# A gMLP and SwiGLU layer on one core: tiles moved to multiples of 512 bytes in SBUF, with the split weights' slots 64 bytes apart in the line

## The chip, the cores and the metric

The kernel runs on one core of one Trainium2 chip. What counts is the device time of one execution in microseconds (us). Kernels are compared by the median of several executions.

## The reference

One layer with batch 1, sequence 2048 and model width 1024, in float32. A conditioning vector c gives shifts, scales and gates.

```
mod = silu(c) @ mod_w + mod_b
sh1, sc1, g1, sh2, sc2, g2 = split(mod, 6)
h = x * (1 + sc1) + sh1
z = gelu(h @ w_in + b_in); u, v = split(z, 2); v = layer_norm(v)
sv = einsum('gts,bnsgc->bntgc', tril(w_s), chunks of 128 of v) + b_s
y = (u * sv) @ w_out
x = layer_norm(2 ** 0.25 * x + (1 + g1) * y)
h = x * (1 + sc2) + sh2
g, u = split(h @ ffn_w_in, 2); y = (silu(g) * u) @ ffn_w_out        (hidden width 2816)
x = layer_norm(2 ** 0.25 * x + (1 + g2) * y)
```

## The kernel before

Every large product is carried in float32 by three passes. An operand is split into two float32r parts, hi and lo, and hi*hi + hi*lo + lo*hi is added up in PSUM. The split is `parts` (lines 85 to 90): ScalarE (ACT) casts the float32 source into the first half of a tile (line 88), VectorE (DVE) writes source minus first half into the second half (line 89). Such a tile has the shape `UNIT`, 4096 bytes a partition; `ROW` is 4096 bytes too, `HALF` 2048. Each matmul reads two such tiles from SBUF: the stationary operand, 128 columns by 128 rows, which a weight load brings in ahead, and the moving operand, 512 columns.

The mixer goes over four blocks of 512 tokens (`b` = 0 to 3) in three stages:

- `v_part` (`token_major`, line 192): the stationary operand is `hT`, on the right side of SBUF, the moving one the split weight `wv`, in the pool `w` on the left.
- `us_part` (`feature_major`, line 209): the stationary operand is `wu` (pool `w`, left), the moving one `hT` (right). Between them stand the short spatial products (line 310) and the transposes (line 382).
- `y_part` (`token_major`, line 192): the stationary operand is `yT`, the moving one `wo` (pool `w`). Both are on the left.

The feed-forward part takes Winograd's form, seven products for a 2x2 one. In `ffn_in` (line 428) the split weights of the pool `w` (left) are stationary and the activations move: A11 and A12 lie on the right, the five others (A22, S1 to S4) on the left. `ffn_in` goes twice over 11 pairs (`f_0` to `f_10`, each with a `g` and a `u` half); a pair has 14 products of 12 matmuls. In `ffn_out` (`mm`, line 577) the moving operand is the split `wd` (pool `w`, or `fin` for the last product, where it lies left), the stationary one the split `al`: for the first half of the tokens in the pool `w` on the right, for the second half in `w2` on the left.

A pool stands for one tag of `phase` (lines 61 to 68). It is a stack with a left side, which grows from the low addresses, and a right side, which grows down from the top:

```
            p = st.enter_context(tc.tile_pool(name=f"{tag}{n[0]}", bufs=bufs, side=side, reuse_waits="tile"))
```

```
    late = phase("left", late=(12, ROW))
    mix = phase("left", w=(7, UNIT), cact=(1, ROW))
    early = phase("right", hT=(8, UNIT), u=(5, HALF), xh=(2, HALF), sv=(2, HALF))
    rest = phase(
        "left", s=(4, HALF), opsS4=(2, UNIT), opsS2=(4, UNIT), h3=(4, ROW), c=(8, HALF), w=(6, UNIT), opsS1=(4, UNIT),
    )
    most = phase("right", ld=(9, HALF), w=(10, UNIT))
```

All slots are multiples of 512 bytes, so all of these tiles on one side have the same place in a line of 512 bytes. That place is 64 on the left and 480 on the right; it follows from the small tiles that are allocated first, and the pads of the change show it (64 + 448 and 480 - 480 are multiples of 512). When a phase ends, its bytes are used again, and `reuse_waits="tile"` makes a new tile wait for the old tiles whose bytes it covers. A scheduler that simulates the program then sets the order of the instructions on each engine; each engine works through its own in order. All loads and stores are issued from SyncE's queue (SP).

Of the kernel before, what the change touches and what calls it, by code (L numbers as in the profile page):

```python
# [8 lines left out]
F32 = mybir.dt.float32  # L9
# [4 lines left out]
P = 128  # L14
# [4 lines left out]
NT = TB // P  # L19
ND = D // P  # L20
NK = ND // 2
NP = 11
ALPHA = 2.0 ** 0.25
EPS = 1e-5

# Winograd's form of the 2x2 product C = A B in seven products:
#   P1 = A11 B11   P2 = A12 B21   P5 = S1 T1   P6 = S2 T2   P3 = S4 B22   P7 = S3 T3   P4 = A22 T4
#   S1 = A21 + A22   S2 = S1 - A11   S3 = A11 - A21   S4 = A12 - S2
#   T1 = B12 - B11   T2 = B22 - T1   T3 = B22 - B12   T4 = B21 - T2
#   C11 = P1 + P2         C12 = P1 + P6 + P5 + P3  # L30
#   C21 = P1 + P6 + P7 + P4   C22 = P1 + P6 + P7 + P5
A_OF = {1: "A11", 2: "A12", 3: "S4", 4: "A22", 5: "S1", 6: "S2", 7: "S3"}
# [4 lines left out]
def gmlp_swiglu_layer(  # L37
# [6 lines left out]
):  # L44
    """One gMLP + SwiGLU layer.

    Every large product is float32 carried as three one-pass products: an operand is the exact
    sum of two float32r parts (12 significant bits each), hi and lo, and hi*hi + hi*lo + lo*hi
    is accumulated in float32. The products of the feed-forward part take Winograd's form.
    """  # L50
    nc = tc.nc
# [4 lines left out]
    dram = ctx.enter_context(tc.tile_pool(name="dram", bufs=1, space=bass.MemoryType.DRAM))  # L56

    ROW, HALF, UNIT = ([P, D], F32), ([P, 512], F32), ([P, 2, 512], F32R)
    cur, n = {}, [0]

    def phase(side, **tags):
        """Open one pool for each tag: tag=(number of slots, shape and type). Close what is returned."""
        st = ExitStack()
        for tag, (bufs, kind) in tags.items():
            n[0] += 1
            p = st.enter_context(tc.tile_pool(name=f"{tag}{n[0]}", bufs=bufs, side=side, reuse_waits="tile"))
            cur[tag] = (p, kind)
        return st

    def new(tag, name, kind=None):  # L70
        p, (shape, dt) = cur[tag][0], kind or cur[tag][1]
        return p.tile(shape, dt, tag=tag, name=name)

    lo, hi = slice(0, 512), slice(512, 1024)
# [10 lines left out]
    def parts(src, name, tag):  # L85
        """[P, 512] float32 as its hi and lo parts."""
        o = new(tag, name, UNIT)
        nc.scalar.copy(out=o[:, 0, :], in_=src)  # L88
        nc.vector.tensor_tensor(out=o[:, 1, :], in0=src, in1=o[:, 0, :].bitcast(F32), op=ALU.subtract)  # L89
        return o  # L90
# [7 lines left out]

    # constants
    ident = const.tile([P, P], F32, name="ident")  # L100
# [5 lines left out]

    # conditioning: mod = silu(c) @ mod_w + mod_b, one column per 128 outputs
    modc = const.tile([P, 48], F32, name="modc")
# [29 lines left out]
    def spread(k, name):  # L138
        """Columns [P, 1] * ND as one row on every partition, by way of DRAM."""
        line = dram.tile([ND, P], F32, name=f"{name}_line")  # L140
        nc.sync.dma_start(out=line.rearrange("d p -> p d"), in_=modc[:, k * ND : (k + 1) * ND])
        t = new("late", name)
        nc.sync.dma_start(out=t, in_=line.rearrange("d p -> (d p)").partition_broadcast(P))
        return t
# [4 lines left out]
    def norm_of(st, name):  # L149
        """Mean and 1 / sqrt(var + EPS)."""  # L150
        mv = small.tile([P, 2], F32, tag="mv", name=f"{name}_mv")
        nc.vector.bn_aggr(out=mv, in_=st)
        ve = small.tile([P, 1], F32, tag="ve", name=f"{name}_ve")
        nc.vector.tensor_scalar(ve, mv[:, 1:2], EPS, None, ALU.add)  # L154
        rs = small.tile([P, 1], F32, tag="rs", name=f"{name}_rs")
        nc.gpsimd.tensor_tensor(out=rs, in0=ve, in1=mhalf, op=ALU.pow)  # L156
        # one Newton step: rs * (1.5 - 0.5 * ve * rs^2)
        nw = small.tile([P, 1], F32, tag="nw", name=f"{name}_nw")
        nc.vector.scalar_tensor_tensor(out=nw, in0=rs, scalar=ve, in1=rs, op0=ALU.mult, op1=ALU.mult)
        nc.vector.tensor_scalar(nw, nw, -0.5, 1.5, ALU.mult, ALU.add)  # L160
        nc.vector.tensor_tensor(out=rs, in0=rs, in1=nw, op=ALU.mult)
        return mv[:, 0:1], rs
# [10 lines left out]
    def ahead(makers, depth=2):  # L173
        """The makers' results in order; each is made `depth` uses before its own."""
        made = [m() for m in makers[:depth]]

        def results():
            for i in range(len(makers)):
                if i + depth < len(makers):
                    made.append(makers[i + depth]())  # L180
                yield made[i]

        return results()

    def token_major(operands, nk, name, between=()):
        """out[t, :] over NT token tiles: sum over k of a_k[:, t].T @ w_k, in all 8 banks."""
        ps = [[bank(f"{name}_ps{t}{h}") for h in range(2)] for t in range(NT)]
        for k, (a, w) in enumerate(operands):
            for t in range(NT):
                for part, wpart in HL:  # L190
                    for h in range(2):
                        nc.tensor.matmul(  # L192
                            ps[t][h],
                            lhsT=a[:, part, t * P : (t + 1) * P],
                            rhs=w[h][:, wpart, :],
                            start=(k == 0 and part == 0 and wpart == 0),
                            stop=(k == nk - 1 and part == 1),
                        )
            for f in between[k :: nk]:
                f()  # L200
        return ps

    def feature_major(w, rhs, name):
        """out[j, tokens] of 128 features: w is [d, (d-tile, j)] in parts."""
        ps = bank(name)
# [13 lines left out]
    x1d = [dram.tile([TB, D], F32, name=f"x1d{b}") for b in range(NB)]  # L219
    # left operands of the feed-forward products, [k, tokens of one half] in float32  # L220
    hop = [[[dram.tile([P, TB], F32, name=f"hop{o}_{k}_{sb}") for sb in range(2)] for k in range(NK)] for o in range(7)]
# [8 lines left out]
    sh1, sc1, g1, sh2, sc2, g2 = ([None] * ND for _ in range(6))  # L230
    env = {}

    def setup_spatial():
        # masked w_s, transposed to [s, (g, t)]
        wm = new("bcv", "wm")
# [3 lines left out]
            out=wm3, in_=wm3,  # L239
            pattern=[[0, 8], [1, P]], compare_op=ALU.is_ge, fill=0.0, base=0, channel_multiplier=-1,  # L240
        )
        # tb[c, (g, t)] = ln_b[c] * sum_s w[t, s] + b_s[g, t]
        lb = new("raw", "lnb_bc")
# [122 lines left out]
    def h2_part(b, i, cols_of, tag):  # L366
        """Transposed, modulated feature tiles i and NK + i; with the second half of a super-block their left operands.

        cols_of(t, q) is token tile t's columns of feature tile i + q * NK.
        """  # L370
        sb = b // 2
# [28 lines left out]
    def a_operands(r0, r1, name):  # L400
        """Raw [k0, (t0, t1)] and [k1, (t0, t1)] -> S1..S4 and the seven left operands in float32."""
        a11, a21, a12, a22 = r0[0], r0[1], r1[0], r1[1]
# [7 lines left out]
    def load_ops(sb, names):  # L410
        def tag_of(n, k):
            """A22, S3 and most of S4 take rows that the mixer leaves."""
            return "late" if n in ("A22", "S3") or (n == "S4" and k > 1) else "ops" + n

        out = {}
# [8 lines left out]
    def ffn_in(sb, ops, between={}):  # L424
# [12 lines left out]
        def weight(fp, pr, gu):  # L437
# [6 lines left out]
            b11, b12, b21, b22 = B[gu]  # L444
            # T1, T2 take the place of B11, T3 of B12, T4 of B21
            if pr == 5:
# [13 lines left out]
        for fp in range(NP):  # L460
            X, Y, Z, c1, u1, u2 = {}, {}, {}, {}, {}, {}
            for pr in order:
# [30 lines left out]
                if (fp, pr) in between:  # L493
                    between[fp, pr]()
            # C11 in c1, C12 in u1, C22 in u2, C21 in X
            for cc in (c1, u2, u1):
# [8 lines left out]
    def residual(b, t, r, cs, st, scaled=False):  # L505
        """r * (1 + g2) + alpha * x1 on half a row, with its sums."""
        xt = new("xr", f"xr{b}_{t}_{cs.start}")[:, : cs.stop - cs.start]
# [10 lines left out]
    def finish(b, t, r, st, e):  # L518
        """Norm and store of one token tile; `e` adds, or none where the wait for it would be the longest."""
        row = b * TB + t * P  # L520
# [15 lines left out]

    # token tile pairs: (sb, p) joins tile p of the first and of the second half of sb
    prs = [(sb, p) for sb in range(2) for p in range(NT)]
# [44 lines left out]
    def ffn_out():  # L583
# [29 lines left out]

        # P3 adds to P5 and P6, P7, P4 to P1 where they accumulate; the last product of the second half
        # comes pair by pair, so that each pair's norm follows at once
        steps = [(pr, k) for pr in (2, 5, 3, 1, 6, 7, 4) for k in range(NP)]
# [153 lines left out]
```

## Time and profile before

| | |
|---|---|
| median of 3 executions | 1949.47 us |
| fastest, slowest | 1949.44 us, 1951.29 us |
| span of the profiled execution, first to last instruction | 1948.5 us |
| median less the span: what lies around it | 1.0 us |
| TensorE (PE) busy | 1875.5 us, 96% of the span |
| DVE, ACT, GpSimd (POOL) busy | 66%, 39%, 37% |
| DMA queue of SP | 47.2% of 16 engines |

The page of the profile takes one execution, and gives no time of its own but the span. A busy PE is not one at its peak: matmuls follow each other in a pipeline, so the distance from one start to the next is what a matmul costs, and the chain of work that ended last gives it, as a run's time by its number of matmuls.

### The profile page before, as it was taken

The page shows a single profiled execution, that of the slowest core. Times are in us where ns is not written, and L with a number is a line of the kernel's source. Part 1 is how long each engine was busy: PE and PEld are TensorE (multiplying, and loading weights), DVE is VectorE, ACT ScalarE, POOL GpSimd, SP SyncE. Part 2 cuts the span into 40 slices and gives each one's busy share as a digit, 9 for nine tenths or more (in the row PEclk, how much of TensorE's full clock was granted, in tenths as well). Part 3 has the DMA queues.
Part 4 walks back from the last instruction along what each step waited for, and adds up shares of the span by engine and source line. Part 5 has one row for each costly group of instructions (what it writes and reads, how often), then busy time and mean ns, then how long its engine had stood idle before and what let it go on. Part 6 is the DMA issues. An engine that isn't in the chain of part 4 may idle for free.

```text
span 1948.5 us, 23471 instructions
## 1 busy us (share of the span) xinstructions
PE 1875.5 (96%) x8297; PEld 1532.5 (79%) x8297; DVE 1284.1 (66%) x1855; ACT 760.2 (39%) x1251; POOL 716.6 (37%) x465
## 2 busy tenths in 40 slices
PE   7999999999999999999999999999999999999776
PEld 6787788778888788888887888888888888887655
DVE  8486866786758856555668566556554433476998
ACT  3432552543545434333345333333343443332321
POOL 0000500550402666645544554355431200244834
PEclk9999999999999999999999999999999999999978
DMA  9358546464455444542236323322347644555542
GB/s 355 121 184 304 170 153 229 156 226 155 141 184 184 140 157 152 173 142 97 103 117 195 121 102 106 108 91 103 113 145 246 215 130 140 168 172 172 191 151 108
DMA packets 135064, 312.77 MB, mean 161 GB/s; under 512 B 16641, under 2 KB 21025, under 8 KB 134946
## 3 DMA queue, kind: packets, MB, share of 16 engines
q1 hardware_dynamic: 134882, 311.24, 47.2%
q8 instruction: 65, 1.06, 0.2%
q14 instruction: 53, 0.43, 0.1%
q0 software_dynamic: 64, 0.03, 0.0%
HBM read 239.37 MB, written 71.84 MB: 160 GB/s over the span
## 4 chain that ended last, share of the span: by engine, by line
PE 80%; DVE 11%; DMA 4%; issue 2%; POOL 1%; ACT 1%; SPq 0%; DVEq 0%; POOLq 0%; ACTq 0%
PE o L577 18%; PE v_ps L192 8%; PE u_ps L209 7%; PE y_ps L192 6%; PE f_4u_X L428 1%; PE f_2u_X L428 1%; PE f_5u_X L428 1%; PE f_3u_X L428 1%; PE f_8u_X L428 1%; PE f_7u_X L428 1%; PE f_6u_X L428 1%; PE f_8g_X L428 1%; PE f_7g_X L428 1%; PE f_6g_X L428 1%; PE f_3g_X L428 1%
## 5 line engine op out<-in xcount | busy, mean ns | idle before, releaser
L577 PE MATMUL o<-wd_w,alw 128*128 128x512 f32 (+1 forms) x1881 | 434.4, 393 | 33.3 <-DVE o L77 28.2
L577 PEld LDWEIGHTS o<-wd_w,alw 128*128 128x128 f32 x1881 | 352.8, 191 | 114.8 <-ACT alw L88 23.5
L192 PE MATMUL v_ps<-wv,hT 128*128 128x512 f32 x768 | 184.8, 402 | 16.7 <-ACT wv L88 11.8
L89 DVE TENSOR_TENSOR alw<-al,alw 128x512 fp32r<-128x512 f32 x154 | 130.1, 877 | 98.0 <-ACT alw L88 97.8
L192 PEld LDWEIGHTS v_ps<-wv,hT 128*128 128x128 f32 x768 | 147.1, 192 | 53.5 <-ACT wv L88 12.1
L209 PE MATMUL u_ps<-hT,wu 128*128 128x512 f32 x768 | 186.5, 402 | 1.8 <-DVE v L281 1.3
L192 PE MATMUL y_ps<-wo,yT 128*128 128x512 f32 x768 | 175.7, 390 | 1.9 <-DVE sv L315 1.9
L209 PEld LDWEIGHTS u_ps<-hT,wu 128*128 128x128 f32 x768 | 144.9, 191 | 36.9 <-issue 1.9
L192 PEld LDWEIGHTS y_ps<-wo,yT 128*128 128x128 f32 x768 | 143.7, 188 | 32.3 <-issue 1.8
L156 POOL TENSOR_TENSOR ln_rs<-ln_ve,mhalf 128x1 f32<-128x1 f32 x32 | 27.8, 876 | 361.2 <-DVE ln_ve L154 349.9
L88 ACT CAST alw<-al 128x512 fp32r<-128x512 f32 x154 | 88.8, 618 | 149.2 <-PE o L577 121.6
L89 DVE TENSOR_TENSOR wu<-wu_raw,wu 128x512 fp32r<-128x512 f32 x64 | 65.8, 1042 | 53.6 <-ACT wu L88 53.5
L80 POOL TENSOR_TENSOR chain<-wd,chain 128x512 f32<-128x512 f32 x22 | 33.7, 1532 | 159.4 <-DVE wd_w L89 127.2
L88 ACT CAST wv<-wv_raw 128x512 fp32r<-128x512 f32 x64 | 37.5, 619 | 106.0 <-PE v_ps L192 43.2
L118 DVE SCALAR_TENSOR_TENSOR modw<-modw,cact 128x1024 f32<-128x1024 f32 x48 | 58.3, 1217 | 19.9 <-DMA modw<-in_modwT 19.9
L89 DVE TENSOR_TENSOR wv<-wv_raw,wv 128x512 fp32r<-128x512 f32 x64 | 47.4, 759 | 22.4 <-ACT wv L88 22.2
L89 DVE TENSOR_TENSOR wo<-wo_raw,wo 128x512 fp32r<-128x512 f32 x64 | 46.4, 732 | 20.4 <-ACT wo L88 20.2
L89 DVE TENSOR_TENSOR wd_w<-wd,wd_w 128x512 fp32r<-128x512 f32 x44 | 34.8, 791 | 37.0 <-ACT wd_w L88 37.0
L88 ACT CAST wo<-wo_raw 128x512 fp32r<-128x512 f32 x64 | 38.6, 616 | 43.5 <-PE y_ps L192 42.1
L88 ACT CAST wu<-wu_raw 128x512 fp32r<-128x512 f32 x64 | 38.2, 616 | 36.1 <-PE v_ps L192 20.8
L88 ACT CAST wd_w<-wd 128x512 fp32r<-128x512 f32 x44 | 27.2, 619 | 48.1 <-PE o L577 36.0
L359 POOL TENSOR_TENSOR r<-r,ln1g_bc 128x1024 f32<-128x1024 f32 x16 | 41.5, 2611 | 11.5 <-ACT r L168 11.5
(604 smaller groups left out, 3879.7 us busy)
## 6 DMA issues: line engine op xcount, KB each, us to landing
al<-aop SPq DMA_DIRECT2D x154, 256.0 KB, 3.2
wd<-in_wd SPq DMA_DIRECT2D x99, 256.0 KB, 3.2
modw<-in_modwT SPq DMA_DIRECT2D x48, 512.0 KB, 8.4
aop<-aop_s SPq DMA_DIRECT2D x88, 256.0 KB, 2.0
wv_raw<-in_wv SPq DMA_DIRECT2D x32, 512.0 KB, 4.6
wu_raw<-in_wu SPq DMA_DIRECT2D x32, 512.0 KB, 4.3
wo_raw<-in_wo SPq DMA_DIRECT2D x32, 512.0 KB, 3.5
hop<-h SPq DMA_DIRECT2D x40, 256.0 KB, 3.1
```

The source lines that it names most:

```text
L80: nc.gpsimd.tensor_tensor(out=o, in0=a, in1=b, op=ALU.subtract)
L88: nc.scalar.copy(out=o[:, 0, :], in_=src)
L89: nc.vector.tensor_tensor(out=o[:, 1, :], in0=src, in1=o[:, 0, :].bitcast(F32), op=ALU.subtract)
L118: nc.vector.scalar_tensor_tensor(out=w, in0=w, scalar=1.0, in1=env["cact"], op0=ALU.mult, op1=ALU.mult, accum_out=modc[:, j : j + 1],)
L156: nc.gpsimd.tensor_tensor(out=rs, in0=ve, in1=mhalf, op=ALU.pow)
L192: nc.tensor.matmul(ps[t][h], lhsT=a[:, part, t * P : (t + 1) * P], rhs=w[h][:, wpart, :], start=(k == 0 and part == 0 and wpart == 0), sto ...
L209: nc.tensor.matmul(ps, lhsT=w[d // 4][:, wpart, (d % 4) * P : (d % 4 + 1) * P], rhs=rhs[d][:, part, :], start=(n == 0), stop=(n == 3 * ND ...
L359: nc.gpsimd.tensor_tensor(out=r, in0=r, in1=env["ln1g"], op=ALU.mult)
L428: nc.tensor.matmul(ps, lhsT=w[:, wpart, k * P : (k + 1) * P], rhs=a[k][:, part, :], start=(first and k == 0 and wpart == 0 and part == 0), ...
L577: nc.tensor.matmul(ps[:, cs], lhsT=a[:, part, p * P : (p + 1) * P], rhs=w[:, wpart, cs], start=(first and part == 0 and wpart == 0), stop= ...
```

## The change

Two pads are allocated ahead of the phases' pools, 448 bytes on the left and 480 on the right, and filled once by DVE. With them the two sides begin at 0 modulo 512. A slot of a pool with the tag `w` grows from 4096 to 4160 bytes, of which the first 4096 are used; its seven (mixer), six (`ffn_in`) and ten (`ffn_out`) slots so lie 0, 64, 128, ... bytes into the line. The pools `w2` and `fin` keep their slots. Tiles behind the pool `w` on its side are moved by its number of slots times 64 bytes: 448 for the mixer's `yT`, `raw`, `bcv` and `vrow`, 384 for `opsS1`. The scratch of the software DMA queue goes from its default of 16384 bytes to 4096, a multiple of 512 less. Comments are taken out; lines from 58 on have other numbers (88 and 89 become 99 and 100, 428 becomes 439).

```diff
+    for side, pad in (("left", 448), ("right", 480)):
+        pads = ctx.enter_context(tc.tile_pool(name=f"pad_{side}", bufs=1, side=side))
+        nc.vector.memset(pads.tile([P, pad // 4], F32, name=f"pad_{side}"), 0.0)
...
     def new(tag, name, kind=None):
         p, (shape, dt) = cur[tag][0], kind or cur[tag][1]
+        if (shape, dt) == UNIT and tag in STEP:
+            t = p.tile([P, 2 * 512 + STEP[tag] // 4], dt, tag=tag, name=name)
+            return t[:, : 2 * 512].rearrange("p (h c) -> p h c", h=2)
         return p.tile(shape, dt, tag=tag, name=name)
+
+    STEP = {"w": 64}
...
-    nc = bacc.Bacc("TRN2", target_bir_lowering=False, num_devices=1)
+    nc = bacc.Bacc("TRN2", target_bir_lowering=False, num_devices=1, dynamic_dma_scratch_size=4096)
```

The matmuls, splits and transfers are the same in number and size. In the built programs' addresses, of 7,881 float32r matmuls those whose two operands differ in their place modulo 512 bytes are:

| | matmuls | before: differ | by | after: differ | by |
|---|---|---|---|---|---|
| v | 768 | 768 | 416 | 648 | 128 to 448 in steps of 64 |
| u | 768 | 768 | 96 | 648 | 64 to 384 |
| y | 768 | 0 | | 768 | 64 to 448 |
| ffn_in | 3696 | 1056 | 96 | 3168 | 64 to 448 |
| ffn_out | 1881 | 1014 | 96, 416 | 1566 | 64 to 448 |
| sum | 7881 | 3606 | | 6798 | |

("By" is the stationary operand's place less the moving one's, modulo 512.)

The order moves in one place only, from the mixer's last product to the first pairs of `ffn_in`, where slots of 4160 bytes lie over other old tiles than before. ACT there, before (`wo_7` is the last weight of the mixer; `h2S` are S1 to S4, whose raw tiles end in the product's name and the feature tile, as `h2S1r_0`; `f_0g_w` is a split weight of the first pair):

```order
393 L88 CAST h2S_0_0_5289<-h2S1r_0_5287 128x512
394 L88 CAST h2S_0_1_5294<-h2S1r_1_5292 128x512
395 L88 CAST wo_7_1_5133<-wo_7_raw 128x512
396 L88 CAST f_0g_w_5331<-f_0g_b_5327 128x512
397 L88 CAST h2S_0_2_5299<-h2S1r_2_5297 128x512
398 L88 CAST f_0u_w_5338<-f_0u_b_5334 128x512
399 L88 CAST f_0g_w_5341<-f_0g_b_5328 128x512
400 L88 CAST f_0u_w_5344<-f_0u_b_5335 128x512
401 L88 CAST h2S_0_3_5304<-h2S1r_3_5302 128x512
402 L88 CAST f_0g_w_5348<-f_0g_b_5327 128x512
403 L88 CAST f_0u_w_5367<-f_0u_b_5334 128x512
404 L88 CAST h2S_0_0_5309<-h2S2r_0_5307 128x512
```

ACT there, after:

```order
393 L99 CAST h2S_0_0_5299<-h2S1r_0_5297 128x512
394 L99 CAST h2S_0_1_5304<-h2S1r_1_5302 128x512
395 L99 CAST wo_7_1_5143<-wo_7_raw 128x512
396 L99 CAST h2S_0_2_5309<-h2S1r_2_5307 128x512
397 L99 CAST h2S_0_3_5314<-h2S1r_3_5312 128x512
398 L99 CAST h2S_0_0_5319<-h2S2r_0_5317 128x512
399 L99 CAST h2S_0_1_5324<-h2S2r_1_5322 128x512
400 L99 CAST f_0g_w_5341<-f_0g_b_5337 128x512
401 L99 CAST f_0u_w_5348<-f_0u_b_5344 128x512
402 L99 CAST f_0g_w_5351<-f_0g_b_5338 128x512
403 L99 CAST f_0u_w_5354<-f_0u_b_5345 128x512
```

The first pair's weights stood ahead of the casts from `h2S2r` (the raw tiles of S2) and now stand behind two of them. The tile that the second of these writes covers part of the slot of `wo_7_0`. PE there, before, with all twelve matmuls of a product together:

```order
1972 L192 MATMUL y_ps_4967<-wo_7_1_5133,yT_7_4925 128x512
1973 L428 MATMUL f_0g_X<-h2A_0_0_5210,f_0g_w_5331 128x512 x3
1974 L428 MATMUL f_0g_X<-h2A_0_1_5215,f_0g_w_5331 128x512 x3
1975 L428 MATMUL f_0g_X<-h2A_0_2_5220,f_0g_w_5331 128x512 x3
1976 L428 MATMUL f_0g_X<-h2A_0_3_5225,f_0g_w_5331 128x512 x3
1977 L428 MATMUL f_0u_X<-h2A_0_0_5210,f_0u_w_5338 128x512 x3
```

PE there, after:

```order
1972 L203 MATMUL y_ps_4977<-wo_7_1_5143,yT_7_4935 128x512
1973 L439 MATMUL f_0g_X<-h2A_0_0_5220,f_0g_w_5341 128x512 x2
1974 L439 MATMUL f_0u_X<-h2A_0_0_5220,f_0u_w_5348 128x512 x2
1975 L439 MATMUL f_0g_Y<-h2A_0_0_5240,f_0g_w_5351 128x512 x2
1976 L439 MATMUL f_0g_X<-h2A_0_0_5220,f_0g_w_5341 128x512
1977 L439 MATMUL f_0g_X<-h2A_0_1_5225,f_0g_w_5341 128x512 x3
1978 L439 MATMUL f_0g_X<-h2A_0_2_5230,f_0g_w_5341 128x512 x3
1979 L439 MATMUL f_0g_X<-h2A_0_3_5235,f_0g_w_5341 128x512 x3
1980 L439 MATMUL f_0u_Y<-h2A_0_0_5240,f_0u_w_5354 128x512 x2
```

The matmuls that need only the hi part of a weight are now taken out of three products and put ahead, since the lo parts come later: on DVE they stand behind the eight multiplications that empty the mixer's banks (line 343 before, 354 after), where the first six stood ahead of them.

## Rows read from the trace of the kernel before

**Rows 1.** The page: span, busy PE, the chain that ended last.

```profile
span 1948.5 us, 23471 instructions
PE 1875.5 (96%) x8297; PEld 1532.5 (79%) x8297; DVE 1284.1 (66%) x1855; ACT 760.2 (39%) x1251; POOL 716.6 (37%) x465
PE 80%; DVE 11%; DMA 4%; issue 2%; POOL 1%; ACT 1%; SPq 0%; DVEq 0%; POOLq 0%; ACTq 0%
```

**Rows 2.** Chain in order of time, mixer: start us, us, what, number.

```profile
274.29 43.55 PE y_ps L192 x192
...
465.86 44.80 PE v_ps L192 x192
510.65 22.50 PE u_ps L209 x96
...
566.29 43.32 PE y_ps L192 x191
```

**Rows 3.** Chain, `ffn_in`, second time, pair 6 and the start of pair 7.

```profile
1281.45 2.81 PE f_6u_X L428 x12
1284.26 2.81 PE f_6g_Y L428 x12
1287.08 2.80 PE f_6u_Y L428 x12
...
1292.62 2.72 PE f_6u_Z L428 x12
1295.35 2.72 PE f_6g_X L428 x12
...
1319.95 2.81 PE f_7u_X L428 x12
```

**Rows 4.** Stretches: us, busy by engine, PEclk (granted clock), DMA share, GB/s.

```profile
319.00:359.00 40.00, 40.00 (x174) 32.16 (x173) 36.65 (x76) 13.54 (x20) 14.26 (x8) 1.00 0.62 214
...
570.00:606.00 36.00, 36.00 (x160) 29.84 (x159) 21.35 (x28) 15.96 (x29) 7.33 (x5) 1.00 0.56 177
1283.00:1450.00 167.00, 167.00 (x730) 136.80 (x729) 98.22 (x105) 60.91 (x104) 80.61 (x52) 1.00 0.32 110
```

**Rows 5.** Groups on ACT: the casts of line 88, busy us, mean ns.

```profile
L88 ACT CAST alw<-al 128x512 fp32r<-128x512 f32 x154 | 88.8, 618 | 149.2 <-PE o L577 121.6 <-DMA al<-aop 18.0 <-issue 6.6
L88 ACT CAST wo<-wo_raw 128x512 fp32r<-128x512 f32 x64 | 38.6, 616 | 43.5 <-PE y_ps L192 42.1 <-PE u_ps L209 1.3
L88 ACT CAST yT<-sv 128x512 fp32r<-128x512 f32 x32 | 19.9, 621 | 48.0 <-DVE sv L322 48.0
```

**Rows 6.** Chain, `ffn_out`: its long stretches of PE, and one between them.

```profile
1477.81 293.32 PE o L577 x1270
...
1814.41 2.89 DVE alw L89
...
1866.42 41.51 PE o L577 x164
```

**Rows 7.** Timeline, end of the mixer: start us, us, engine, line, instruction.

```profile
596.04 0.68 DVE L89 TENSOR_TENSOR f_0g_w<-f_0g_b,f_0g_w 128x512 fp32r<-128x512 f32 x1
...
604.88 0.68 DVE L89 TENSOR_TENSOR f_0u_w<-f_0u_b,f_0u_w 128x512 fp32r<-128x512 f32 x1
605.56 5.37 DVE L343 TENSOR_TENSOR r<-y_ps,g_bc 128x512 f32<-128x512 f32 x8
605.96 0.62 ACT L88 CAST h2S<-h2S2r 128x512 fp32r<-128x512 f32 x1 [3.78 <-DMA h2S2r<-hop]
...
609.66 2.97 PE L428 MATMUL f_0g_X<-h2A,f_0g_w 128*128 128x512 f32 x12
```

**Rows 8.** Waits of PE from 600 to 720 us: us in total, times, longest.

```profile
PE f_1u_Y L428 <- DVE f_1u_w L89: 3.0, 1, 3.0
PE f_1g_Y L428 <- DVE f_1g_w L89: 0.9, 1, 0.9
PE f_1g_Y L428 <- ACT f_1g_w L88: 0.8, 1, 0.8
```

**Rows 9.** Chain, the first piece: what the start waits for.

```profile
2.20 7.67 DMA xT<-in_xT
```

## The prediction

> **What bounds the kernel now.** The page comes first: PE is busy 96% of the span, and 80% of the chain that ended last is PE's own work [rows 1]. So the next question is what one matmul costs inside a stretch where PE waits for nothing. The chain in order of time gives it, as a run's time by its number of matmuls. The reader should see two prices there, and no third. In `y`, where both operands lie on the left, 192 matmuls take 43.55 us, or 226.8 ns each, and 191 take 43.32, again 226.8 [rows 2]. In `v` it is 44.80 / 192 = 233.3 ns and in `u` 22.50 / 96 = 234.4 ns [rows 2]; there one operand is on the right. `ffn_in` has both prices side by side, in one loop: the products with A11 and A12, whose activations lie on the right, take 2.81 us for twelve (234.2 ns), those with S1 to S4 and A22 take 2.72 us (226.7 ns) [rows 3]. [...]
>
> What goes with the price? In the dear matmuls the stationary and the moving operand stand at 64 and 480 in a line of 512 bytes, in the cheap ones at the same place. Distance does not order them: by the built program's addresses the cheap products with A22 reach further through SBUF (from about 20,000 to 157,000) than the dear ones (from 135,000 to 229,000). Which side an operand is on does not by itself do it either, since in the built program the first half of `ffn_out` has both operands at 480. [...] Other engines don't care: ACT's casts take 616 ns with source and target at 64, 618 in the mixed group, 621 from 480 to 64 [rows 5].
>
> **The change, part by part.** *The pads* remove the difference between the sides. *The 64-byte steps* bring a new one, between any slot of the pool `w` but the first and whatever stands at 0, and between two slots in `ffn_out`. Moreover seven slots of 64 bytes push the mixer's `yT` to 448, where none of its seven `wo` slots stands. By the table of addresses, 3,606 matmuls have operands at different places before, and 6,798 after. The differences are no longer 96 and 416 but multiples of 64, and no row shows the price of one. The nearest rows are the two differences that are there: 6.5 ns over the cheap price (`v`, 416) and 7.6 (`u`, 96) or 7.5 (`ffn_in`, 96). [...] The high end I put at 8.7 ns, as far beyond 7.6 as that is beyond 6.5. I take 7.0, the middle of what was measured, because 96 and 416 lie inside the span from 64 to 448 that the steps cover, and on both its flanks the price is nearly the same. That speaks for a level, reached as soon as the places differ, rather than for a slope.
>
> The sum, on the path that sets the end:
> - `y`: 768 matmuls go from equal to different places, 768 x 7.0 ns = 5.4 us.
> - `ffn_in`: 3168 - 1056 = 2112 more, 14.8 us. A pair, 38.50 us from 1281.45 to 1319.95 [rows 3], should take 39.1.
> - `ffn_out`: PE carries the chain for 29 + 1270 matmuls and for the last 164 [rows 6]. In the first 1299 the built programs have 649 different pairs before and 1132 after, so 483 x 7.0 = 3.4 us; in the last 164 it is 91 in both. The matmuls between (some 70 more differ) lie in a stretch where the chain runs through DVE's splits and other engines, one split of 2.89 us among them [rows 6]; they cost nothing there, and would cost 0.5 us without that cover.
> - `v` and `u`: 120 fewer each, 120 x 6.5 + 120 x 7.6 = 1.7 us back.
>
> That is 5.4 + 14.8 + 3.4 - 1.7 = 21.9 us.
>
> *The new order at the end of the mixer.* Before, the first six lo parts of `ffn_in` are done by 605.56, before DVE empties the banks for 5.37 us, and PE begins `f_0g_X` at 609.66 with all it needs [rows 7]. After, ACT casts S2's second tile ahead of `f_0g_w`. That tile covers bytes of `wo_7_0`, which PE reads until the mixer's last matmuls, just before 609.66. So ACT stands in front of it, with the weights of the first pair queued behind; two casts of 0.62 us follow before PE has a first hi part, at about 610.9. DVE comes out of the banks at 610.93, does two lo parts of S2 and then that of `f_0g_w`, three of about 0.68: 613.0. Until then PE has six matmuls; before, it had done (613.0 - 609.66) / 0.234 = 14. It loses eight, or 2 us. If the waits of PE behind it, 3.0 + 0.9 + 0.8 us for the weights of the next pair [rows 8], take in this delay, the loss is nothing; if DVE's queue passes it on to them, they grow by about as much again, and with the norms queued there I put the high end at 6. I take 2.
>
> *The rest:* two fills of 112 and 120 columns stand first on DVE, under the first load of 7.67 us [rows 9]; without that cover they would cost well under 1 us. The smaller scratch serves two small loads and moves nothing else. DVE, ACT and POOL get no instruction more, and PE being slower, their cover grows.
>
> Against the profiled execution: 1948.5 + 21.9 + 2 = 1972.4 us of span; with the 1.0 us around it the median goes from 1949.5 to **1973 us**. With one of the seven steps free of charge it would be 7 us less (6798 / 7 x 7.0 ns) and with the high ends of price (8.7 ns also on the 1296 of `v` and `u`: 8 us) and order (4 us) 12 more, so the forecast's own range is 1966 to 1985. About 0.2%, 4 us, is what a measurement of this kernel can tell from no change.
>
> [...] The same instructions take 2.81 or 2.72 us, by where their operands lie [rows 3]. [...]
>
> **The rivals.**
> - *A multiple of 64 is harmless* (faster). 64 and 480 also differ by 32 modulo 64, so all rows would fit a rule with 64 bytes in place of 512. Then the steps do nothing, the pads do everything, and the prices of today fall away: 768 x 6.5 + 768 x 7.6 + 1056 x 7.5 + (649 + 91) x 7.0 ns = 23.9 us, less 2 for the order: 1928 us (1924 to 1932). For it: nothing in the trace excludes it. [...] It decides from a mean price of the new differences of (23.9 - 2) / 6455 matmuls on the path = 3.4 ns: below that the change wins. Chance 0.18.
> - *Some steps cost, others do not.* With half the price, 3.5 ns, 6455 x 3.5 = 22.6 us come and 23.9 go: 1950 us, from about 1938 to 1962. For it: 416 and 96 are not quite equal. Chance 0.16.
> - *Places have no say* and something else goes with A11, A12, `v` and `u`. Then only the order is left: 1951.5 us. [...] Against it stands `ffn_in` [rows 3], with equal instructions in one loop, and the mixer's two prices. Chance 0.08.
> - [...] No row has a matmul of 512 columns under 226 ns in a run, so 0.04.
>
> **How the numbers follow.** The forecast has 0.54. Faster by over 0.2%: 0.18 + 0.04 + 0.06 of the mixed case = 0.28. Within 0.2%: 0.08 + 0.05 = 0.13. Slower: 0.54 + 0.05 = 0.59. The range reaches down to the first rival and up to near the high end of the forecast, 1926 to 1980; outside stay the last rival and the outer ends of the others, about 0.15.
>
> **What would show it.** In the chain, `y` should rise from 43.55 to 44.9 us for 192 matmuls; in `ffn_in` products on the right and on the left should read alike, 2.81 us, and 2.72 only where the weight's slot is the first of six; `v` and `u` should hardly move. A wait of PE of some 2 us should stand at about 611 us. Wrong it is if `y` stays at 226.8 ns per matmul (the first rival), or if the twelve matmuls of one product take different times by slot (the second).

## The result, and the profile after

The changed kernel takes 1971.73 us (median of 4, from 1967.98 to 1974.64), the kernel before 1949.45 us beside it (median of 4): a ratio of 1.011, with an interval of 1.009 to 1.0131. The profiled execution takes 1972.5 us with a span of 1970.8, 22.3 us above the span of before. The forecast was 1973. The page of the kernel after, span, busy time and chain, against [rows 1]:

```profile
span 1970.8 us, 23470 instructions
PE 1893.3 (96%) x8297; PEld 1540.7 (78%) x8297; DVE 1267.5 (64%) x1857; ACT 760.0 (39%) x1251; POOL 725.0 (37%) x465
PE 80%; DVE 13%; DMA 3%; issue 2%; POOL 1%; ACT 1%; SPq 0%; DVEq 0%; POOLq 0%; ACTq 0%
```

PE is busy 17.8 us longer for the same matmuls (a spell at the lower clock, below, is in it), and the rest is waiting. The chain in order of time of the kernel after (start us, us, what, number) shows the price of the places, against [rows 2, 3, 6]:

```profile
271.41 44.46 PE y_ps L203 x192
315.87 44.32 PE v_ps L203 x192
360.19 22.20 PE u_ps L220 x96
...
1302.37 2.80 PE f_6u_X L439 x12
1305.17 2.76 PE f_6g_Y L439 x12
...
1316.25 2.74 PE f_6g_X L439 x12
...
1500.66 293.83 PE o L588 x1270
```

`y` rose from 226.8 to 231.6 ns per matmul (from start to start; by itself a matmul of `y` lasts 390 ns on the mean in the trace of before, so they overlap), `v` and `u` fell a little, to 230.8 and 231.3, and the products of `ffn_in` lie anywhere from 2.73 to 2.80 us for twelve, by slot: from nearly the old cheap price (2.72) to nearly the dear one (2.81). The other part of the loss stands in one stretch. The waits of PE from 600 to 720 us in the kernel after (total us, times, longest), against [rows 8]:

```profile
PE f_0u_X L439 <- DVE f_0u_w L100: 4.5, 1, 4.5
PE f_1g_Y L439 <- DVE f_1g_w L100: 2.5, 1, 2.5
PE f_1g_Y L439 <- ACT f_1g_w L99: 1.8, 1, 1.8
PE f_0g_X L439 <- DVE h2A L100: 1.8, 1, 1.8
PE f_0u_Z L439 <- DVE f_0u_w L100: 1.2, 1, 1.2
PE f_0g_X L439 <- ACT f_0g_w L99: 1.0, 1, 1.0
PE f_0g_X L439 <- DVE f_0g_w L100: 0.2, 1, 0.2
```

That is 13.0 us where it was 4.7. And the clock granted to PE falls in it. Stretches of the kernel after (us, busy by engine, granted clock, DMA share, GB/s):

```profile
626.00:634.00 8.00, 5.87 (x24) 4.36 (x24) 8.00 (x9) 4.78 (x8) 3.84 (x2) 1.00 0.03 8
634.00:642.00 8.00, 4.68 (x11) 3.72 (x12) 8.00 (x14) 2.92 (x7) 0.00 (x0) 0.59 0.16 37
642.00:656.00 14.00, 14.00 (x61) 11.43 (x61) 12.19 (x33) 6.43 (x9) 8.61 (x8) 0.99 0.62 204
```

Around the end of its wait of 4.5 us PE is granted 0.59 of its clock from 634 to 642 us, and from 637 to 642, where it works again, 0.50. DVE, meanwhile, is busy without a gap from 626 to 642 us, and PE's wait ends with a lo part from it.

### The profile page after: what moved, and what is told of

The parts are those of the page before. It is cut to its first block, busy times and chain, and to the rows that moved or that the text cites. A ratio compares the mean times of both kernels' runs of the same rounds, so it can differ in the third digit from the quotient of the medians.

```text
span 1970.8 us, 23470 instructions
## 1 busy us (share of the span) xinstructions
PE 1893.3 (96%) x8297; PEld 1540.7 (78%) x8297; DVE 1267.5 (64%) x1857; ACT 760.0 (39%) x1251; POOL 725.0 (37%) x465
## 4 chain that ended last, share of the span: by engine, by line
PE 80%; DVE 13%; DMA 3%; issue 2%; POOL 1%; ACT 1%; SPq 0%; DVEq 0%; POOLq 0%; ACTq 0%
PE o L588 17%; PE u_ps L220 7%; PE v_ps L203 7%; PE y_ps L203 7%; DVE modw L129 1%; PE f_2u_X L439 1%; PE f_5u_X L439 1%; PE f_8u_X L439 1%; PE f_7u_X L439 1%; PE f_4u_X L439 1%; PE f_6u_X L439 1%; PE f_3u_X L439 1%; PE f_7g_X L439 1%; PE f_4g_X L439 1%; PE f_3g_X L439 1%
## 5 line engine op out<-in xcount | busy, mean ns | idle before, releaser
L100 DVE TENSOR_TENSOR alw<-al,alw 128x512 fp32r<-128x512 f32 x154 | 124.8, 843 | 98.6 <-ACT alw L99 98.6
L203 PE MATMUL y_ps<-wo,yT 128*128 128x512 f32 x768 | 182.1, 399 | 2.8 <-DVE sv L326 2.8
L100 DVE TENSOR_TENSOR wu<-wu_raw,wu 128x512 fp32r<-128x512 f32 x64 | 59.4, 945 | 52.1 <-ACT wu L99 51.7
L99 ACT CAST wv<-wv_raw 128x512 fp32r<-128x512 f32 x64 | 37.5, 619 | 104.0 <-PE v_ps L203 41.0
L100 DVE TENSOR_TENSOR wv<-wv_raw,wv 128x512 fp32r<-128x512 f32 x64 | 47.6, 763 | 22.7 <-ACT wv L99 22.6
```

The costliest lines, as they stand in the source:

```text
L203: nc.tensor.matmul(ps[t][h], lhsT=a[:, part, t * P : (t + 1) * P], rhs=w[h][:, wpart, :], start=(k == 0 and part == 0 and wpart == 0), sto ...
```

## The experiments

Three theories stood at the start. **A** is the prediction's: places count modulo 512 bytes, every unequal place costs 7 ns, the new order 2 us. **B**: they count modulo 256 or less and cost 0 to 6 ns, and the order at the mixer's end costs some 15 us. **C**: places have no say. The edits below are against the changed kernel.

**The pads alone, and 512 in place of 64.** The first leaves out the steps (and has the order of before), the second keeps the changed kernel's order and puts all operands at 0 modulo 512.

```diff
-    STEP = {"w": 64}
+    STEP = {}
```

> The pads and the smaller scratch stay, the 64-byte steps are taken out: all 7,881 float32r matmuls have both operands at the same place in the line, and the order at the end of the mixer is that of the kernel before. Theory A (the forecast: every unequal place costs some 7 ns a matmul, the new order 2 us): the 23.9 us of the kernel before go, 1925 to 1927 us. Theory B (unequal places cost 0 to 6 ns by their distance, and the new order about 15 us): the same 1925 to 1927 us, with u at 96 matmuls in 21.8 us and y unchanged at 43.5 for 192. Theory C (places have no say): 1949 us.

```diff
-    STEP = {"w": 64}
+    STEP = {"w": 512}
```

> Steps of 512 bytes in place of 64: all operands at the same place in the line again, but the slots lie over other old tiles, and the order at the end of the mixer is that of the changed kernel. It prices the order by itself, against the kernel with pads alone. Theory A: 2 us more than pads alone, 1927 to 1929 us. Theory B: about 15 us more, 1938 to 1943 us, with the waits of PE between 600 and 720 us at 13 us in place of 4.7. Theory C: the order is all there is, 1970 us.

Measured: the pads alone take 1928.87 us against 1946.92 for before beside it, a ratio of 0.991 (0.9896 to 0.9924), span 1927.6; that is a little over the 1925 to 1927 that A and B expected. With 512 a step it is 1946.94 us, 1.0002 (0.999 to 1.0015), span 1940.7. Chain of the kernel with the pads alone:

```profile
462.55 43.52 PE v_ps L203 x192
506.07 21.84 PE u_ps L220 x96
560.37 43.32 PE y_ps L203 x191
```

`v` now costs 226.7 ns and `u` 227.5, like `y`. So places do decide (C falls), and the order by itself costs 13 us of span, 18 by the medians, at the same price per matmul (the span is that of the fastest of the twelve executions with 512 a step). Theory B's 15 us lies between. The waits of PE from 600 to 720 us in the kernel with 512 a step begin like those of the changed kernel, and sum to 13.9 us; with the pads alone the sum is 3.8:

```profile
PE f_0u_X L439 <- DVE f_0u_w L100: 4.6, 1, 4.6
PE f_1g_Y L439 <- DVE f_1g_w L100: 2.5, 1, 2.5
PE f_1g_Y L439 <- ACT f_1g_w L99: 2.5, 1, 2.5
```

**The price by distance.** Without steps, the right pad alone sets one distance for all matmuls that have an operand on each side. (In the first expectation below the count of 4,600 should read 3,606, as in the table ahead of the prediction.)

```diff
-    for side, pad in (("left", 448), ("right", 480)):
+    for side, pad in (("left", 448), ("right", 224)):
...
-    STEP = {"w": 64}
+    STEP = {}
```

> Pads alone, but the right side's pad is 224 in place of 480, so that its tiles stand at 256 in the line: v, u, A11 and A12 and a part of ffn_out (4,600 matmuls in all... those that were unequal before) are 256 apart, the order is that of before. Theory A, where a line has 512 bytes: 233 to 234 ns in v, u, A11, A12, as before, and 1948 to 1951 us. Theory B, where the distance counts modulo 256: 226.8 ns everywhere, and the time of pads alone, 1925 to 1927 us. Theory C: 1949 us.

With 352 in place of 224 the right tiles begin at 128, with 416 at 64, with 288 at 192, with 448 at 32:

> Pads alone with the right side at 128 in the line: v is 128 apart, u, A11 and A12 384, a part of ffn_out either; order as before. Theory A: 233 to 234 ns in these, 1948 to 1951 us. Theory B, from the changed kernel's matmuls at 128 and 384: about 232.5 ns, 1944 to 1948 us; v and u read alike, because 128 and 384 are the same modulo 256. Theory C: 1949 us, with the prices of before.

> The right tiles are put at 64 and the left ones at 0, no steps. Places then differ by 64 in v and by 448 in u and in the products with A11 and A12 of ffn_in. If the line repeats every 256 bytes and only the distance within it counts, 448 is the same as 192. Theory B1 (price by distance within 256, read from the mixed kernel): v about 232.5 ns per matmul, u and A11/A12 about 230.5. Theory B2 (any distance but 0 and 256 costs the same): 232.5 to 234 for all. Left products of ffn_in 2.72 us for twelve under either.

> The mirror image: right tiles at 192, so 192 in v and 320 in u and A11/A12; 320 is 64 within 256. Theory B1: v about 230.5 ns, u and A11/A12 about 232.5. Theory B2: all 232.5 to 234. If right64 and right192 swap their prices between v and u, the sign of the difference counts; if each keeps its price by the smaller distance on the circle of 256, it does not.

> The right tiles at 32, the left ones at 0, no steps: v differs by 32, u and the products with A11 and A12 by 480, which is 224 modulo 256. Measured so far over the price of equal places, modulo 256: 64 costs 6.5 ns, 96 7.4, 128 5.8, 160 6.5, 192 2.2. If the price falls off towards a whole 256 (theory A2, a line in which only the part still ahead counts), u and A11/A12 take 227 to 228.5 ns per matmul and v 232 to 234. If 192 is low because it is a multiple of 64 and what counts is another grid, 224 costs as much as 96 and 160, 233 to 234. Left products of ffn_in 2.72 us for twelve under either.

The chains of these kernels, `v` (192 matmuls) and `u` (96). Right tiles at 256:

```profile
462.81 43.52 PE v_ps L203 x192
506.33 21.87 PE u_ps L220 x96
```

At 128:

```profile
463.59 44.63 PE v_ps L203 x192
508.22 22.40 PE u_ps L220 x96
```

At 64:

```profile
462.76 44.80 PE v_ps L203 x192
507.56 21.99 PE u_ps L220 x96
```

At 192:

```profile
466.87 43.95 PE v_ps L203 x192
510.81 22.40 PE u_ps L220 x96
```

At 32:

```profile
465.75 44.80 PE v_ps L203 x192
510.55 22.40 PE u_ps L220 x96
```

Worked out per matmul, over 226.7 ns for `v` and 227.5 for `u` at equal places (the row at 96 and 416 is from [rows 2]):

| stationary less moving, modulo 256 | from | over the price of equal places |
|---|---|---|
| 0 (256 modulo 512) | `v`, `u` | 0.0, 0.3 ns |
| 32 | `v` | 6.6 |
| 64 | `v`; `u` (320) | 6.6; 5.8 |
| 96 | `u` | 6.9 |
| 128 | `v`; `u` (384) | 5.7; 5.8 |
| 160 | `v` (416) | 6.6 |
| 192 | `v`; `u` (448) | 2.2; 1.6 |
| 224 | `u` (480) | 5.8 |

The price repeats after 256 bytes, which ends theory A: 256 apart costs 0.0 and 0.3 ns, and 64 and 320, 128 and 384, 192 and 448 each go together. At the distances measured between, the price is a level of 5.7 to 6.9 ns, with one exception, 192, at a third (1.6 to 2.2). The sign of the difference counts, since 64 and 192 are mirror images and cost 6.6 and 2.2. Theory A2, by which 224 would be cheap as well, was wrong: it costs 5.8. The kernel with 256 apart takes 1932.31 us (0.9925, 0.9908 to 0.9942), with 128 apart 1945.16 (0.999, 0.9981 to 1.0); one execution each of those with 64, 192 and 32 took 1936.21, 1945.96 and 1948.73. All these kernels have the smaller scratch, the dear ones too, so it is the places that gain in the pads alone, and not the scratch.

**256 a step.** The change with `STEP = {"w": 256}`, to see whether 0 and 256 may also be mixed within a loop.

> The change with 256 bytes a step in place of 64: its order, and all places 0 or 256 apart. If 256 is as good as 0 also where distances are mixed, every matmul takes 226.8 ns and the span is that of the kernel with 512 a step, 1941 us within 4; if mixing itself costs, equal places rise to about 229 ns and the span to about 1955.

Measured: 1944.12 us, 0.9988 (0.9979 to 0.9998), span 1941.1, with 2.72 us for twelve matmuls of `ffn_in` and 43.52 for `v`. Mixing 0 and 256 costs nothing here: with 512 a step these take 2.72 and 43.52 us too, in a span of 1940.7.

Mixing equal and unequal places is not quite free. Before, `f_6g_Z` has both operands at 64, yet directly behind the dear `f_6u_Y` [rows 3] it takes 2.75 us and not 2.72:

```profile
1289.88 2.75 PE f_6g_Z L428 x12
```

It is 2.75 in each of the pairs 1 to 10 of the second half. In the changed kernel `f_6g_Y` and `f_6g_X` above, 2.76 and 2.74 us, have equal places modulo 256 by the built program's addresses and stand behind dear products. Why some of the price runs on into the next product no run shows.

**The two halves.** Steps of 64 only in the feed-forward pools, and steps of 512 only in the mixer's pool.

```diff
-    STEP = {"w": 64}
+    STEP = {}
...
     mix.close()
+    STEP["w"] = 64
```

> The pads, and the steps of 64 bytes only in the feed-forward pools, none in the mixer. The mixer's tiles then lie as in the kernel with the pads alone, so the order at the mixer's end should be that of before, and the two causes come apart. Prices by distance modulo 256, from the kernels with one distance each: 64 costs 6.5 ns, 128 6.0, 192 2.2. Of the feed-forward matmuls 1470 stand at 64, 1398 at 128 and 1041 at 192: 9.6 + 8.4 + 2.3 = 20 us over the span of the pads alone, 1927.6, so 1948 (theory A2: prices by distance, order from the mixer's pool). With one level price of 7.0 ns it would be 27 us, 1955. If the order's loss came from the steps in the feed-forward pool, the waits of PE from 600 to 720 us would be 13 us again and the span 1961.

```diff
-    STEP = {"w": 64}
+    STEP = {"w": 512}
...
     mix.close()
+    STEP.clear()
```

> The other half: 512 a step in the mixer's pool alone, none in the feed-forward pools; every matmul at equal places. If moving the mixer's seven slots is what turns the order, the waits of PE from 600 to 720 us are 13 to 14 us and the span is 1941, as with 512 everywhere; if it is the feed-forward slots, waits are 4 us and the span 1928.

The first takes 1946.42 us (1.0, 0.9989 to 1.0011), span 1943.5: 15.9 us over the pads alone where 20 were expected, and 17.3 by the medians, each less the before beside it. Waits of PE from 600 to 720 us in it:

```profile
PE f_1u_Y L439 <- DVE f_1u_w L100: 3.1, 1, 3.1
PE f_1g_Y L439 <- ACT f_1g_w L99: 1.2, 1, 1.2
PE f_1g_Y L439 <- DVE f_1g_w L100: 0.9, 1, 0.9
```

These are the waits of before [rows 8]. The second takes 1945.11 us (0.9988, 0.9979 to 0.9998), span 1945.6, with 15.6 us of such waits, `f_0u_X` for 4.5 us at their head. In the traces the first has the order of before on PE, ACT, DVE and GpSimd, and the second that of 512 a step. So the order turns because the mixer's seven slots move, and not by the feed-forward pool; the two costs come apart.

**What in the new order costs it.** S2 of the first half is loaded later, which takes its casts away from ahead of the first pair's weights on ACT (512 a step throughout):

```diff
-    ops.update(load_ops(0, ("S1", "S2")))
+    ops.update(load_ops(0, ("S1",)))
...
-    between[0, 1] = lambda: (ops.update(load_ops(0, ("S3", "A22"))), norm(0), norm(1))
+    between[0, 1] = lambda: (ops.update(load_ops(0, ("S2", "S3", "A22"))), norm(0), norm(1))
```

> 512 a step, and S2 of the first half is loaded and split after the first pair's X and Y products instead of before ffn_in, so that ACT no longer stands in front of S2's second tile (which covers wo_7_0) with the first pair's weights behind it. On DVE the first pair's lo parts still stand behind the eight multiplications that empty the mixer's banks. Theory H (ACT's place in front of S2 is the cause of the loss): waits of PE from 600 to 720 us fall from 13.9 to about 5 and the span from 1940.7 to 1930 or less. Theory K (DVE's order is the cause, with the lo parts and the norms queued ahead of the weights): waits stay at 10 to 13 us and the span at 1937 to 1940.

Measured: 1946.62 us, 0.9996 (0.9984 to 1.0009), span 1945.0, and 14.0 us of waits. The gain that theory H expected did not come, and the ranges of K were passed as well. The test is not a clean one. Two of its waits do not stand among those of 512 a step, one for a tile of S4 (`f_0g_Z`) and one for a tile of S2 (`f_0g_X`), which now come late:

```profile
PE f_0g_Z L439 <- DVE h2S L100: 2.7, 1, 2.7
PE f_0g_X L439 <- DVE h2S L100: 2.1, 1, 2.1
```

Without them 9.2 us would be left, so H is not excluded as a part of the loss. The timeline of this kernel (start us, us, engine, line, instruction, idle time before it and what ended it) shows what stayed:

```profile
597.84 5.37 DVE L354 TENSOR_TENSOR r<-y_ps,g_bc 128x512 f32<-128x512 f32 x8 [5.60 <-PE y_ps L203]
...
603.12 0.68 DVE L100 TENSOR_TENSOR f_0g_w<-f_0g_b,f_0g_w 128x512 fp32r<-128x512 f32 x1
...
603.88 1.68 POOL L91 TENSOR_TENSOR f_0g_b<-f_0g_b 128x512 f32<-128x512 f32 x1 [86.11 <-DVE f_0g_w L100]
```

ACT had cast the weight at 591.42, but the lo part stands behind the emptying of the banks on DVE, which sits idle for 5.60 us until the mixer's last matmuls are done. And GpSimd (POOL) waits for the lo part too: `weight` writes the differences of Winograd's form over the loaded weight (`sub(b11, b12, b11)`), so the difference may not begin before DVE has read that half. In the kernel after:

```profile
605.24 5.49 DVE L354 TENSOR_TENSOR r<-y_ps,g_bc 128x512 f32<-128x512 f32 x8 [5.62 <-PE y_ps L203]
...
610.63 0.73 PE L439 MATMUL f_0g_X<-h2A,f_0g_w 128*128 128x512 f32 x2 [0.99 <-ACT f_0g_w L99]
...
612.61 1.68 POOL L91 TENSOR_TENSOR f_0g_b<-f_0g_b 128x512 f32<-128x512 f32 x1 [89.49 <-DVE f_0g_w L100]
...
623.53 0.62 ACT L99 CAST f_0g_w<-f_0g_b 128x512 fp32r<-128x512 f32 x1 [4.98 <-POOL f_0g_b L91]
...
637.32 4.63 PE L439 MATMUL f_0u_X<-h2S,f_0u_w 128*128 128x512 f32 x10 [4.52 <-DVE f_0u_w L100]
```

With the pads alone the same difference starts thus (POOL's timeline):

```profile
590.71 1.29 POOL L91 TENSOR_TENSOR f_0g_b<-f_0g_b 128x512 f32<-128x512 f32 x1 [71.12 <-DVE f_0g_w L100]
```

There `f_0g_X` begins at 603.7: GpSimd has a lead of 13 us. In the changed kernel it comes 2 us after PE, and ACT's next casts wait for it, 4.98 us for one, until PE in its turn waits 4.52 for `f_0u_w`. The last kernel takes that tie away: the first pair's differences get tiles of their own, with 512 a step. The rest of the program is as it was, but the scheduler, free of the tie, also orders ACT, DVE and PE anew from about 604 us on.

```diff
+            if pr in (5, 6) and (sb, fp) == (0, 0):
+                own = new("diff", f"{nm}_t{pr}")
+                sub(own, b12 if pr == 5 else b22, b11)
+                b11 = own
+                B[gu] = b11, b12, b21, b22
-            if pr == 5:
+            elif pr == 5:
                 sub(b11, b12, b11)
```

(`diff` is a pool of four `HALF` tiles at the end of `rest`.)

> 512 a step, its order at the mixer's end, but the first pair's four differences (B12 - B11 and B22 - T1, for g and u) are written to tiles of their own and not over the loaded weight. GpSimd then need not wait for DVE's lo parts of that weight, which stand behind the emptying of the banks: in the kernel with 512 a step its first difference starts 2 us after the first matmul of ffn_in, in the kernel with the pads alone 13 us before it. Theory P (GpSimd's late start carries the delay on to the later products of the first pair): the waits for f_0u_w, 4.6 and 1.3 us, fall away or shrink to under 2 us together, and the span falls from 1940.7 to 1933 to 1936. Theory D (DVE itself is the bound: it idles 5.6 us ahead of the banks' emptying and then has more than it can do): the waits move to other products but their sum stays at 11 to 15 us, and the span at 1938 to 1943.

Measured: 1937.93 us, 0.9941 (0.9926 to 0.9957), span 1932.8. The waits of PE from 600 to 720 us:

```profile
PE f_1g_Y L439 <- ACT f_1g_w L99: 4.4, 1, 4.4
PE f_1g_Y L439 <- DVE f_1g_w L100: 2.0, 1, 2.0
PE f_0g_X L439 <- DVE h2A L100: 1.8, 1, 1.8
PE f_0g_X L439 <- ACT f_0g_w L99: 1.0, 1, 1.0
PE f_0g_X L439 <- DVE f_0g_w L100: 0.2, 1, 0.2
```

The waits for `f_0u_w` are gone, as theory P has it, and with them 8 us of span, 10.6 by the medians, each less the before beside it. GpSimd now writes the first difference at 565.84, before ACT casts that weight at 602.37. The first pair, from its first matmul to that of the next, takes 29.3 us, with 512 a step 37.5 and with the pads alone 28.6. What is left, 9.4 us of waits and a span 5.2 us above that of the pads alone, has moved on to the second pair, where D would have it. Taking the tie away, with the order that this allowed, brought back the larger share; how much is GpSimd's start alone and how much the new order was not taken apart. The rest is DVE's, or that of the loads behind it. Which of the old tiles that the new layout covers makes the scheduler choose this order stays open as well: S2's second tile is not it alone, since the order of DVE stayed when S2 was moved away.

**The faster version** is the one with the pads alone, 1928.87 us: 0.9% faster than before, and 2% under the change.

## Why the prediction was right, point by point

The time was right to 1.3 us, but by luck: two terms of the working were off by some 10 to 20 us each, against one another.

**That places set the price** held. The same matmuls cost 226.7 or 233.3 ns when nothing but a pad differs. The rival by which places have no say falls. The clock is not the cause, as it is 1.00 in stretches of either price [rows 4]. Why unequal places cost more no run shows. Of the other engines only ACT's casts were read, 616 to 621 ns at three pairings of places [rows 5].

**"A level, reached as soon as the places differ"**, at 7.0 ns for all 6,798 matmuls, is the first term that failed. The level was nearly right (5.7 to 6.9 ns), but not for each distance. By the built program 2,166 of the 7,815 matmuls with 512 columns now stand at equal places modulo 256, 2,010 at 64, 2,082 at 128 and 1,557 at 192: 2,010 x 6.6 + 2,082 x 5.7 + 1,557 x 2.2 ns = 28.6 us. The changed kernel against the one with 512 a step, same order, is 30.1 us of span, and 22.3 us by the medians, each less the before beside it. At 7.0 ns the 6,798 would cost 47.6. Going from the places of before, which cost 20.9 us of span (18.1 by the medians, the pads alone), the net of the places is about 9 us by the spans, 4 by the medians, and not 21.9. Term by term, from the traces:

- `y`, forecast +5.4: 192 matmuls take 0.91 us more, four times that is 3.6.
- `ffn_in`, forecast +14.8 or 0.6 a pair: from the third pair of the first half to the start of `ffn_out` the lag behind before grows from 14.9 to 22.6 us, 7.7 us in 20 pairs, 0.39 each.
- `ffn_out`, forecast +3.4: 1270 matmuls take 293.83 for 293.32 us, +0.5. At equal places (512 a step) they take 287.88, so the unequal ones of before cost 5.4 us in all and the nearly twice as many of after 6.0: here too the price was no level.
- `v` and `u`, forecast -1.7: 0.48 us less four times and 0.3 eight times, -4.3. They "should hardly move", and did gain.

Together these are 7.5 us.

**The new order, forecast +2 with a high end of 6**, is the second. From the first matmul of pair 0 to that of pair 2 it takes 90.0 us where it took 76.0, and some 0.8 of these 14 are places; in the kernels with 512 a step and with the pads alone, at equal prices, it takes 88.9 and 74.3. The step itself, PE's start, was right: PE began at 610.63 (forecast 610.9), the first lo part came at 611.85 to 612.53 (613.0), and PE lost 1.2 us there. What failed is the range for what comes behind, "if DVE's queue passes it on to them, they grow by about as much again": the prediction followed DVE's queue and overlooked GpSimd's, whose in-place differences wait for those lo parts. GpSimd's start, 15 us later against PE, went on through GpSimd, ACT's casts and DVE's next lo parts to the last products of the pair, and PE came out of the wait with 0.50 of its clock granted (637 to 642 us).

**The rivals.** That multiples of 64 are harmless falls by the kernel with 128 apart, at 5.7 ns in `v` and 5.8 in `u`. The mixed one (some steps cost, others do not) was the best description of the places: distances have three prices, and the products of one loop differ, 2.73 to 2.80 us, the sign named for it. Its 1950 us was too low for two reasons: 11 us more for the order make it 1961, and the other 10 come from its sum of places, where it had 22.6 us to come and 23.9 to go and the spans show 30.1 and 20.9. That the steps beat equal places, the last of the rivals (0.04): no stretch of 512-column matmuls in the chains shown here is below 226 ns each, and no run shows a distance cheaper than equal places.

So 21.9 + 2 was forecast; the spans show about +9 and +13, the medians about +4 and +18.

## What to carry to other kernels

Where PE is the bound, compare the time per matmul between loops of the same shape; if it has two values at the same clock, look at the places of the two operands in SBUF, and try them equal modulo 256 (here 21 us of 1949 by the spans, 18 by the medians, for two small pads). Before any edit of tile sizes, compare the order of instructions, and for each one that comes later follow every engine that reads or overwrites its operands: an update in place ties a producer to a reader that the data flow doesn't name (here GpSimd began 2 us behind PE, in place of 13 ahead). And check the terms of a right forecast one by one: here, by the spans, one was more than twice too large and the other a sixth of what it was, and the sum hid it.

## What the runs showed of the hardware that was not expected

- The price of two operands' places repeats after 256 bytes and not after the 512 read from before: 256 apart costs 0.0 to 0.3 ns a matmul. Its sign counts: 64 costs 6.6 ns, 192 only 2.2, with 5.8 to 6.6 on both sides of it (160 and 224).
- After the wait of 4.5 us PE was granted 0.50 of its clock from 637 to 642 us (0.59 from 634), so its next ten matmuls took 4.63 us. With the pads alone the same stage has waits of at most 1.5 us. Over stretches of 20 us from 600 to 720 us the lowest mean clock is 0.91 there and 0.74 in the changed kernel.
- Twelve matmuls at equal places take 2.72 us behind others at equal places, and 2.75 behind a product at unequal ones (pairs 1 to 10 of the second half, before).
